# Four feature-major products written token-major, three groups of merged rows turned by VectorE and DRAM, and the last output weights split during the groups before

## The chip, the core and the metric

The kernel runs on one core of one Trainium2 chip. The metric is the device time in microseconds of one execution; lower is better. A time stands for the median of several executions. The profile is of one further execution, whose own time and whose span (first to last instruction of the program) are given with it.

## The reference

One decoder layer over 256 tokens of width 2048, everything in float32:

```python
h = rms_norm(x, norm_w)
proj = h @ w_in                      # 18464 columns
(sb_q, sb_k, sb_v, sb_z, ssd_z, ssd_xbc, ssd_dt, mem_q, mem_z, gate_pre) = split(proj)
o_sb  = stick_breaking_attention(sb_q, sb_k, sb_v) * silu(sb_z)      # 8 heads of 128
x_ssm, b, c = split(silu(causal_conv(ssd_xbc)))
o_ssd = gated_group_rms_norm(ssd_scan(x_ssm, dt, a, b, c) + d * x_ssm, ssd_z)
o_mem = memory_cross_attention(mem_q, rms_norm(mem), w_mem_kv) * silu(mem_z)  # 4 heads of 256
gates = sigmoid(gate_pre + b_gate)
merged = g_sb*(o_sb @ w_branch_sb) + g_ssd*(o_ssd @ w_branch_ssd) + g_mem*(o_mem @ w_branch_mem)
out = rms_norm(x + merged @ w_out, final_norm_w)
```

Nearly all of the work is weight products over 256 tokens: every weight is read from HBM once and used for 256 rows.

## The kernel before

Each product keeps float32 accuracy by splitting both operands into a high and a low part (`split`, lines 140 to 152). ScalarE (ACT) writes the rounded part `wh` from the loaded chunk `raw` (L146), VectorE (DVE) subtracts and writes the rest, `wl` (L150), and TensorE (PE) adds up three products, high by high, high by low and low by high. A chunk of weights is 128 x 1024 numbers, 512 KB, loaded on SyncE's queue (SP) into one of 4 `raw` buffers; `wh` and `wl` have 3 buffers each.

There are two forms of product.

- `gemm` is token-major. The activations are the stationary operand (128 tokens), 512 columns of the weight stream. A chunk is 2 contraction steps of 128 by 512 columns, and PE does 12 matmuls of 512 on it (L266, L267, L268). The result has tokens on partitions.
- `gemm_cols` is feature-major. 128 columns of the weight are stationary and the tokens stream. A chunk is 4 contraction steps by 256 columns. For each step PE does two matmuls of 512 (L229: the high weight by both parts of the activation, side by side) and two of 256 (L233: the low weight). The result has features on partitions, in two halves that `fold` adds up (L246 on ACT, L247 on DVE).

The attention products, the convolution and the scan need features on partitions. For the gates z of each branch the kernel uses `gemm` and turns the result (`to_turned`): DVE transposes 32 x 32 blocks out of PSUM, ACT's queue writes them to a scratch in DRAM and reads them back in four transfers that put the blocks in place. The merged rows, which the output product needs as its stationary operand, are turned by PE (`merged_cols`, L872), eight transposes for each group of 512 columns, into a PSUM bank, from which they are split.

The order of every engine's work is the order in which the program is written (`manual_schedule`). After each chunk's matmuls `pump` counts one step, calls what was put off to this step (`defer(fn, chunks)`) and takes one step of one of two lanes, in which the small work of the attention heads and the scan waits. So "3 chunks later" is a place in the program. An engine works through its own list in order, and ACT issues its DMAs from the same list.

The stages by time: memory values; memory keys (`kT`, feature-major); memory queries (`qM`, feature-major); the gates z of memory and stick-breaking (token-major, turned); stick-breaking queries and keys (`qS`, `kS`, feature-major), during which the memory heads run in the lanes; its values; the scan's z (turned); the convolution's input (feature-major, not touched); then three times four groups of a gate product and a branch product, whose results are added into `merged`; at last four groups of the output product. The first three of these are `gemm`. For the fourth, the code loads and splits all weights first and then runs 48 matmuls of 512 for the first 128 tokens and twice 48 of 256 for the others, so that the end of the kernel is short.

Of the kernel before, what the change touches and what calls it, by code (L numbers as in the profile page):

```python
# [10 lines left out]
F32 = mybir.dt.float32  # L11
F32R = mybir.dt.float32r
# [29 lines left out]
def trunk_kernel(  # L42
# [19 lines left out]
    def nm(s):  # L62
        cnt[0] += 1
        return f"{s}_{cnt[0]}"
# [7 lines left out]
    def ta(shape, n):  # L72
        return tmp.tile(shape, F32, tag="ta", name=nm(n), bufs=4)
# [10 lines left out]
    def small2(shape, n):  # L84
        return tmp.tile(shape, F32, tag="cu", name=nm(n), bufs=2)

# [85 lines left out]
    def defer(fn, chunks=LATE):  # L172

        cnt[0] += 1
        heapq.heappush(late, (now[0] + chunks, cnt[0], fn))
# [72 lines left out]

    def gemm(lhs, nk, w, c0, evac):

        acc2 = psA.tile([P, 2, GW], F32, tag="acc", name=nm("acc"), bufs=2)
        acc = [acc2[:, 0], acc2[:, 1]]
        kc = KC
        for k0 in range(0, nk, kc):
            raw = load_chunk(w, c0, GW, k0, kc)
            wh = stage.tile([P, kc, GW], F32R, tag="wh", name=nm("wh"))
            wl = stage.tile([P, kc, GW], F32R, tag="wl", name=nm("wl"))
            split((wh, wl, raw, None))
            for j in range(kc):
                kt = k0 + j  # L260
                lh, ll = lhs.at(kt)
                first, last = kt == 0, kt == nk - 1
                for t in range(2):
                    a = acc[t]
                    tt = slice(t * P, (t + 1) * P)
                    nc.tensor.matmul(a, lh[:, tt], wh[:, j], start=first, stop=False)  # L266
                    nc.tensor.matmul(a, lh[:, tt], wl[:, j], start=False, stop=False)  # L267
                    nc.tensor.matmul(a, ll[:, tt], wh[:, j], start=False, stop=last)  # L268
            pump()
        defer(lambda: evac(acc))  # L270
# [26 lines left out]

    def to_turned(dst, g):

        scratch = dram.tile([2, P, 4, 4, 32], F32, name=nm("turned"))  # L300
        cols = dst[:, 4 * g:4 * g + 4].rearrange("p k t -> p (k t)").rearrange(
            "p (i n) -> p i n", n=P)

        def evac(acc):
            for t in range(2):
                blocks = ta([P, 4, 4, 32], "blocks")
                nc.vector.transpose(blocks.rearrange("p j k c -> p k j c"),
                                    acc[t].rearrange("p (k j c) -> p k j c", k=4, j=4))
                defer(lambda t=t, blocks=blocks: nc.scalar.dma_start(
                    scratch[t].rearrange("p j k c -> p (j k c)"),  # L310
                    blocks.rearrange("p j k c -> p (j k c)")), 1)
            defer(back, 3)

        def back():
            for j in range(4):
                nc.scalar.dma_start(
                    cols[32 * j:32 * j + 32],
                    scratch[:, :, j].rearrange("t (i r) k c -> r (t i) (k c)", r=32))
        return evac

    def turned(a, i, n=1):
# [134 lines left out]
    def wait_x(k0):  # L456

        assert len(x_ready) >= k0 // 2 + 2, (k0, x_ready)

# [9 lines left out]
    kT = Cols(8, "kT")  # L469
    for g in range(4):  # L470
        gemm_cols(memT, NKT, w_mem_kv, 2 * g * P, to_split_cols(kT, 2 * g),
                  acc=None if g else [bank([P, 2, T], "acc") for _ in range(2)])
    finish()
# [83 lines left out]
    zS = slot([P, 8, T], F32, "zS")  # L557
    for g in range(4):
        gemm_cols(hT, NKT, w_in, C_MEMQ + 2 * g * P, to_split_cols(qM, 2 * g),
                  ready=None if g else wait_x)  # L560
    for dst, c0 in ((zM, C_MEMZ), (zS, C_SBZ)):
# [69 lines left out]
    for dst, c0 in ((qS, C_SBQ), (kS, C_SBK)):  # L631
        for g in range(4):
            gemm_cols(hT, NKT, w_in, c0 + 2 * g * P, to_cols(dst, 2 * g))
    for g in range(2):
# [249 lines left out]
    def branch_evac(br, g, sig):  # L884
        cs = slice(g * GW, (g + 1) * GW)
        def evac(acc):
            for t in range(2):
                if br == 0:
                    nc.vector.tensor_tensor(merged[t][:, cs], acc[t], sig[:, t], ALU.mult)
                else:  # L890
                    nc.vector.tensor_tensor(sig[:, t], acc[t], sig[:, t], ALU.mult)  # L891
                    nc.gpsimd.tensor_tensor(merged[t][:, cs], merged[t][:, cs], sig[:, t],  # L892
                                            ALU.add)
            if br == 2:
                for pr in range(2):
                    defer(lambda pr=pr: merged_cols(4 * g + 2 * pr), 1)
# [62 lines left out]
    def out_evac(g):  # L959
# [4 lines left out]
        return evac  # L964

    for g in range(3):
        gemm(mT[0], NKT, w_out, g * GW, out_evac(g))
# [3 lines left out]
    xr = x_chunk(g)  # L971
    his, los = [], []
    for k0 in range(0, NKT, KC):
        if k0 % 4 == 0:
            his.append(slot([P, 4, GW], F32R, "wlh"))
            los.append(slot([P, 4, GW], F32R, "wll"))
        raw = load_chunk(w_out, g * GW, GW, k0, KC)
        split((his[-1][:, k0 % 4:k0 % 4 + KC], los[-1][:, k0 % 4:k0 % 4 + KC], raw, None))
    drain()
    for t in range(2):  # L980
        tt = slice(t * P, (t + 1) * P)
        for cs in (slice(0, GW),) if t == 0 else (slice(0, T), slice(T, GW)):
            acc = psA.tile([P, 2, GW], F32, tag="acc", name=nm("acc"),
                           bufs=2)[:, 0, 0:cs.stop - cs.start]
            for kt in range(NKT):
# [49 lines left out]
```

## Time and profile before

| | |
|---|---|
| median of 3 executions | 1226.38 us (1225.35 to 1226.67) |
| profiled execution, its own time | 1225.48 us |
| its span | 1223.7 us |
| PE busy in the span | 99% |
| DVE, ACT, POOL busy | 64%, 52%, 4% |
| memory keys: first matmul to that of the next stage | 52.52 to 98.12 us |
| memory queries | 98.12 to 147.11 us |
| memory's and stick-breaking's z | 147.11 to 235.10 us |
| stick-breaking queries and keys | 235.10 to 335.28 us |
| output product, three groups | 1126.51 to 1192.68 us |
| last output group | from 1192.68 us |

PE's matmuls overlap in the records: the time that one adds is read from the distance between two starts, not from its own duration. What ACT, DVE and SP wait for costs nothing by itself; it costs when PE then waits.

### The profile page before, as it was taken

The page shows a single profiled execution, that of the slowest core. Times are in us where ns is not written, and L with a number is a line of the kernel's source. Part 1 is how long each engine was busy: PE and PEld are TensorE (multiplying, and loading weights), DVE is VectorE, ACT ScalarE, POOL GpSimd, SP SyncE. Part 2 cuts the span into 40 slices and gives each one's busy share as a digit, 9 for nine tenths or more (in the row PEclk, how much of TensorE's full clock was granted, in tenths as well). Part 3 has the DMA queues.
Part 4 walks back from the last instruction along what each step waited for, and adds up shares of the span by engine and source line. Part 5 has one row for each costly group of instructions (what it writes and reads, how often), then busy time and mean ns, then how long its engine had stood idle before and what let it go on. Part 6 is the DMA issues. An engine that isn't in the chain of part 4 may idle for free.

```text
span 1223.7 us, 16119 instructions
## 1 busy us (share of the span) xinstructions
PE 1213.0 (99%) x6132; PEld 1024.1 (84%) x6132; DVE 781.5 (64%) x990; ACT 640.7 (52%) x859; POOL 50.4 (4%) x50
## 2 busy tenths in 40 slices
PE   9999999999999999999999999999999999999997
PEld 7888888888888888888888888888888888888886
DVE  5686564556654555888887758676677755555554
ACT  6764533364444444545665757475756544444443
POOL 0000000000000000010100000000000010110101
PEclk9999999999999999999999999999999999999999
DMA  9966578875466778655668667576856666567673
GB/s 308 364 201 191 156 233 230 244 204 155 149 179 189 223 217 232 183 176 177 177 184 221 208 198 222 180 232 180 233 182 189 204 194 210 185 196 243 201 245 112
DMA packets 169646, 251.07 MB, mean 205 GB/s; under 512 B 11040, under 2 KB 85984, under 8 KB 169440
## 3 DMA queue, kind: packets, MB, share of 16 engines
q1 hardware_dynamic: 151840, 229.51, 61.7%
q10 hardware_dynamic: 17728, 20.53, 5.6%
q8 instruction: 48, 0.79, 0.3%
q14 instruction: 30, 0.25, 0.1%
HBM read 243.68 MB, written 6.32 MB: 204 GB/s over the span
## 4 chain that ended last, share of the span: by engine, by line
PE 96%; DMA 1%; issue 1%; ACT 1%; DVE 1%; SPq 0%; POOLq 0%; POOL 0%; ACTq 0%
PE acc L266 20%; PE acc L267 19%; PE acc L268 19%; PE acc L229 19%; PE acc L233 10%; PE acc L429 1%; PE acc L430 1%; PE acc L428 1%; PE y L806 1%; DMA raw<-in_w_out_dram 1%; DMA raw<-in_w_mem_kv_dram 1%; DVE wl L150 0%; PE dtp L490 0%; PE mt L872 0%; PE xp L763 0%
## 5 line engine op out<-in xcount | busy, mean ns | idle before, releaser
L150 DVE TENSOR_TENSOR wl<-raw,wh 128x1024 fp32r<-128x1024 f32 (+1 forms) x409 | 502.8, 1232 | 327.1 <-ACT wh L146 325.1
L146 ACT ACTIVATE wh<-raw 128x1024 fp32r<-128x1024 f32 (+1 forms) x409 | 431.4, 1056 | 417.8 <-PE acc L268 277.6
L229 PE MATMUL acc<-hT,wh 128*128 128x512 f32 x896 | 282.5, 397 | 0.1
L266 PE MATMUL acc<-wh,hT 128*128 128x512 f32 x704 | 276.6, 393 | 0.0
L267 PE MATMUL acc<-wl,hT 128*128 128x512 f32 x704 | 274.3, 390 | 0.0
L268 PE MATMUL acc<-wh,hT 128*128 128x512 f32 x704 | 274.3, 390 | 0.0
L233 PEld LDWEIGHTS acc<-hT,wl 128*128 128x128 f32 x896 | 168.2, 188 | 40.7 <-DVE wl L150 1.0
L233 PE MATMUL acc<-hT,wl 128*128 128x256 f32 x896 | 176.2, 278 | 0.5 <-DVE wl L150 0.5
L268 PEld LDWEIGHTS acc<-wh,hT 128*128 128x128 f32 x704 | 132.2, 188 | 27.9
L266 PEld LDWEIGHTS acc<-wh,hT 128*128 128x128 f32 x704 | 132.2, 188 | 27.3 <-ACT sq L146 0.5
L267 PEld LDWEIGHTS acc<-wl,hT 128*128 128x128 f32 x704 | 132.3, 188 | 26.8 <-DVE wl L150 0.6
L229 PEld LDWEIGHTS acc<-hT,wh 128*128 128x128 f32 x896 | 136.6, 189 | 0.5 <-ACT wh L146 0.3
L266 PE MATMUL acc<-wh,oD 128*128 128x512 f32 x128 | 49.8, 389 | 0.0
L267 PE MATMUL acc<-wl,oD 128*128 128x512 f32 x128 | 49.8, 389 | 0.0
L268 PE MATMUL acc<-wh,oD 128*128 128x512 f32 x128 | 49.8, 389 | 0.0
L720 DVE SCALAR_TENSOR_TENSOR cT<-cu,wcols,cT 128x255 f32<-128x255 f32 (+2 forms) x96 | 46.4, 483 | 3.4
L892 POOL TENSOR_TENSOR merged<-merged,sig 128x512 f32<-128x512 f32 x16 | 25.1, 1590 | 521.5 <-DVE sig L891 521.5
L229 PE MATMUL acc<-memT,wh 128*128 128x512 f32 x128 | 40.5, 398 | 0.0
L266 PE MATMUL acc<-wh,mT 128*128 128x512 f32 x96 | 37.4, 390 | 0.0
L268 PE MATMUL acc<-wh,mT 128*128 128x512 f32 x96 | 37.4, 389 | 0.0
L267 PE MATMUL acc<-wl,mT 128*128 128x512 f32 x96 | 37.4, 389 | 0.0
L233 PEld LDWEIGHTS acc<-memT,wl 128*128 128x128 f32 x128 | 24.0, 188 | 5.9 <-DVE wl L150 0.3
(245 smaller groups left out, 1280.3 us busy)
## 6 DMA issues: line engine op xcount, KB each, us to landing
raw<-in_w_in_dram SPq DMA_DIRECT2D x288, 512.0 KB, 4.2
raw<-in_w_branch_ssd_dram SPq DMA_DIRECT2D x32, 512.0 KB, 4.3
raw<-in_w_out_dram SPq DMA_DIRECT2D x32, 512.0 KB, 4.9
raw<-in_w_mem_kv_dram SPq DMA_DIRECT2D x31, 512.0 KB, 6.2
raw<-in_w_branch_mem_dram SPq DMA_DIRECT2D x16, 512.0 KB, 3.8
raw<-in_w_branch_sb_dram SPq DMA_DIRECT2D x16, 512.0 KB, 4.8
dec<-acT SPq DMA_DIRECT2D x24, 256.0 KB, 6.4
turned<-blocks ACTq DMA_DIRECT2D x16, 256.0 KB, 4.4
```

The lines of the kernel that those rows point to most:

```text
L146: nc.scalar.activation(hi, src, AF.Copy, **({} if scale is None else {"scale": scale}))
L150: nc.vector.tensor_tensor(lo, src, h32, ALU.subtract)
L229: nc.tensor.matmul(halves[b], wh[:, kt - k0, b * P:(b + 1) * P], lhs.both(kt), start=first, stop=False, skip_group_check=True)
L233: nc.tensor.matmul(halves[b][:, 1], wl[:, kt - k0, b * P:(b + 1) * P], lhs.at(kt)[0], start=False, stop=last, skip_group_check=True)
L266: nc.tensor.matmul(a, lh[:, tt], wh[:, j], start=first, stop=False)
L267: nc.tensor.matmul(a, lh[:, tt], wl[:, j], start=False, stop=False)
L268: nc.tensor.matmul(a, ll[:, tt], wh[:, j], start=False, stop=last)
L428: nc.tensor.matmul(a, lh[:, tt], wh[:, g], start=first, stop=False)
L429: nc.tensor.matmul(a, lh[:, tt], wl[:, g], start=False, stop=False)
L430: nc.tensor.matmul(a, ll[:, tt], wh[:, g], start=False, stop=last)
L720: nc.vector.scalar_tensor_tensor(a[:, s:T], u[:, 0:T - s], convw[:, 3 - s, i:i + 1], a[:, s:T], ALU.mult, ALU.add)
L892: nc.gpsimd.tensor_tensor(merged[t][:, cs], merged[t][:, cs], sig[:, t], ALU.add)
```

## The change

1. **Memory's and stick-breaking's queries and keys.** The 16 calls of `gemm_cols` (four for each of `kT`, `qM`, `qS`, `kS`) become 8 calls of `gemm`. Their rows are turned by the path of the gates z, now a general `turning`: DVE transposes both token halves into one tile `blocks`, ACT issues one write of 512 KB one chunk later, the four reads back 2 chunks after that into a tile `turned`, and 3 chunks later this is split (`split_turned`: `kT`, `qM`) or copied (`copy_turned`: `qS`, `kS`). The turned z go through the same code, with one write of 512 KB where there were two of 256 KB.
2. **Merged rows.** Groups 0 to 2 go through `split_turned` from SBUF; only group 3 is still turned by PE.
3. **The last output group.** Its eight chunks of weights are loaded into a tile `early`, one every three chunks of the three groups before, and split two chunks after each load is issued. Its second token half adds up in PSUM banks of the other pool.
4. The assertion on the scaled x follows the smaller contraction step; a small tile of the scan has a tag of its own; the program's `dynamic_dma_scratch_size` is 1024.

```diff
-    def gemm(lhs, nk, w, c0, evac):
+    def gemm(lhs, nk, w, c0, evac, ready=None, acc=None):
...
-    def to_turned(dst, g):
-        scratch = dram.tile([2, P, 4, 4, 32], F32, name=nm("turned"))
...
-                defer(lambda t=t, blocks=blocks: nc.scalar.dma_start(
-                    scratch[t].rearrange("p j k c -> p (j k c)"),
-                    blocks.rearrange("p j k c -> p (j k c)")), 1)
-            defer(back, 3)
+    def turning(use=None, dst=None):
+        scratch = dram.tile([2, P, 4, 4, 32], F32, name=nm("scratch"))
+        def evac(rows):
+            blocks = tmp.tile([P, 2, 4, 4, 32], F32, tag="blocks", name=nm("blocks"), bufs=1)
             for t in range(2):
+                nc.vector.transpose(blocks[:, t].rearrange("p j k c -> p k j c"),
+                                    rows[t].rearrange("p (k j c) -> p k j c", k=4, j=4))
+            defer(lambda: away(blocks), 1)
+        def away(blocks):
+            nc.scalar.dma_start(scratch.rearrange("t p j k c -> p t (j k c)"),
+                                blocks.rearrange("p t j k c -> p t (j k c)"))
+            defer(back, 2)
         def back():
+            cols = dst
+            if dst is None:
+                cols = tmp.tile([P, 8, P], F32, tag="turned", name=nm("turned"), bufs=1)
             for j in range(4):
                 nc.scalar.dma_start(
                     cols[32 * j:32 * j + 32],
                     scratch[:, :, j].rearrange("t (i r) k c -> r (t i) (k c)", r=32))
+            if use is not None:
+                defer(lambda: use(cols), 3)
         return evac
...
+    def split_turned(dst, g):
+        def use(cols):
+            for k in (0, 2):
+                split((*[blocked(a) for a in dst.at(4 * g + k, 2)], tiles(cols, k, 2), None))
+        return turning(use)
+    def copy_turned(dst, g):
+        return turning(lambda cols: nc.scalar.activation(
+            blocked(dst[:, 4 * g:4 * g + 4]), tiles(cols, 0, 4), AF.Copy))
...
-    for g in range(4):
-        gemm_cols(memT, NKT, w_mem_kv, 2 * g * P, to_split_cols(kT, 2 * g),
-                  acc=None if g else [bank([P, 2, T], "acc") for _ in range(2)])
+    for g in range(2):
+        gemm(memT, NKT, w_mem_kv, g * GW, split_turned(kT, g),
+             acc=None if g else [bank([P, GW], "acc") for _ in range(2)])
...
-        gemm_cols(hT, NKT, w_in, C_MEMQ + 2 * g * P, to_split_cols(qM, 2 * g),
+        gemm(hT, NKT, w_in, C_MEMQ + g * GW, split_turned(qM, g),
...
-            gemm_cols(hT, NKT, w_in, c0 + 2 * g * P, to_cols(dst, 2 * g))
+            gemm(hT, NKT, w_in, c0 + g * GW, copy_turned(dst, g))
...
-            if br == 2:
+            if br == 2 and g < 3:
+                defer(lambda: split_turned(mT[0], g)([merged[t][:, cs] for t in range(2)]), 1)
+            elif br == 2:
                 for pr in range(2):
                     defer(lambda pr=pr: merged_cols(4 * g + 2 * pr), 1)
...
+    early = [slot([P, 4, GW], F32, "early")]
+    def ahead(k0):
...
+        ks = slice(k0 % 4, k0 % 4 + KC)
+        raw, hi, lo = early[0][:, ks], his[-1][:, ks], los[-1][:, ks]
+        nc.sync.dma_start(raw, w_out[k0 * P:(k0 + KC) * P, 3 * GW:].rearrange(
+            "(k p) n -> p k n", p=P))
+        defer(lambda: split((hi, lo, raw, None)), 2)
+    for k0 in range(0, NKT, KC):
+        defer(lambda k0=k0: ahead(k0), 1 + 3 * k0 // KC)
...
-            acc = psA.tile([P, 2, GW], F32, tag="acc", name=nm("acc"),
-                           bufs=2)[:, 0, 0:cs.stop - cs.start]
+            if t == 0:
+                acc = psA.tile([P, 2, GW], F32, tag="acc", name=nm("acc"), bufs=2)[:, 0]
+            else:
+                acc = bank([P, T], "acc")
```

How PE's list changes, at the first contraction step of the memory keys, all 512 columns. Before (`acc_523` and `acc_524` are the two column blocks of 128, and a group covers 256 columns; one row of the memory values stands ahead):

```order
L430 MATMUL acc_145<-wh_497,memT_125 128x512
L229 MATMUL acc_523<-memT_122,wh_527 128x512
L229 MATMUL acc_524<-memT_122,wh_527 128x512
L233 MATMUL acc_523<-memT_122,wl_528 128x256
L233 MATMUL acc_524<-memT_122,wl_528 128x256
```

Now (`acc_524` and `acc_525` are the two halves of the tokens, and a group covers 512 columns):

```order
L457 MATMUL acc_145<-wh_497,memT_125 128x512
L269 MATMUL acc_524<-wh_528,memT_122 128x512
L270 MATMUL acc_524<-wl_529,memT_122 128x512
L271 MATMUL acc_524<-wh_528,memT_122 128x512
L269 MATMUL acc_525<-wh_528,memT_122 128x512
L270 MATMUL acc_525<-wl_529,memT_122 128x512
L271 MATMUL acc_525<-wh_528,memT_122 128x512
```

So two matmuls of 512 and two of 256 for 256 columns have become six of 512 for 512 columns, and the low weight is used second, no longer third.

ACT's list in the stick-breaking keys, around the second pair of memory heads. Before (`kS` rows are the folds out of PSUM, `mpr` the heads' exponentials, `mph` a head's split out of PSUM):

```order
L146 ACTIVATE wh_2840<-raw_2838 128x1024
L146 ACTIVATE wh_2864<-raw_2862 128x1024
L246 ACTIVATE kS_2053<-acc_2714 128x512
L587 ACTIVATE mpr_2835,sums_2890<-mpr_2835,nmx_2888 128x256 x2
L146 ACTIVATE wh_2899<-raw_2897 128x1024
L587 ACTIVATE mpr_2860,sums_2923<-mpr_2860,nmx_2921 128x256 x2
L146 ACTIVATE wh_2932<-raw_2930 128x1024
L146 ACTIVATE wh_2960<-raw_2958 128x1024
```

Now (`scratch` rows write the blocks away, `turned` rows read them back):

```order
L313 DMA scratch_2286<-blocks_2575 128x2x512
L146 ACTIVATE wh_2614<-raw_2612 128x1024
L146 ACTIVATE wh_2634<-raw_2632 128x1024
L322 DMA turned_2650<-scratch_2286 32x8x128 x4
L614 ACTIVATE mpr_2610,sums_2659<-mpr_2610,nmx_2657 128x256 x2
L146 ACTIVATE wh_2668<-raw_2666 128x1024
L614 ACTIVATE mpr_2630,sums_2688<-mpr_2630,nmx_2686 128x256 x2
L146 ACTIVATE wh_2697<-raw_2695 128x1024
L146 ACTIVATE wh_2721<-raw_2719 128x1024
L345 ACTIVATE kS_1929<-turned_2650 128x1024
```

The fold ahead of the exponentials has gone; in its place stand the four reads back, and the copy of 1024 comes two chunks after the exponentials.

ACT's list in the first output group, now (`wlh` rows are the last group's weights, from `early`; before, all eight `wlh` stood behind the three groups):

```order
L146 ACTIVATE wh_9222<-raw_9220 128x1024
L146 ACTIVATE wlh_9199<-early_9177 128x1024
L146 ACTIVATE wh_9246<-raw_9244 128x1024
L146 ACTIVATE wh_9275<-raw_9273 128x1024
L146 ACTIVATE wh_9293<-raw_9291 128x1024
L146 ACTIVATE wlh_9199<-early_9177 128x1024
L146 ACTIVATE mT_8083<-mt_9263 128x2x256
L146 ACTIVATE mT_8083<-mt_9268 128x2x256
L146 ACTIVATE wh_9317<-raw_9315 128x1024
```

One more split of a chunk stands behind every third chunk, the second of them right ahead of the split of the fourth group's merged columns.

More of the change, by code (lines that the diff above doesn't have):

```diff
@@ L84, in small2 @@
     def small2(shape, n):
-        return tmp.tile(shape, F32, tag="cu", name=nm(n), bufs=2)
+        return tmp.tile(shape, F32, tag="cbs", name=nm(n), bufs=2)
     def bank(shape, n="bank"):
@@ L247, in fold @@
             nc.vector.tensor_tensor(dst, acc[:, :, 0], dst, ALU.add)
-    def gemm(lhs, nk, w, c0, evac):
-        acc2 = psA.tile([P, 2, GW], F32, tag="acc", name=nm("acc"), bufs=2)
-        acc = [acc2[:, 0], acc2[:, 1]]
+    def gemm(lhs, nk, w, c0, evac, ready=None, acc=None):
+        if acc is None:
+            acc2 = psA.tile([P, 2, GW], F32, tag="acc", name=nm("acc"), bufs=2)
+            acc = [acc2[:, 0], acc2[:, 1]]
         kc = KC
         for k0 in range(0, nk, kc):
+            if ready is not None:
+                ready(k0)
             raw = load_chunk(w, c0, GW, k0, kc)
@@ L318, in back, with quarter, tiles, to_turned @@
                     scratch[:, :, j].rearrange("t (i r) k c -> r (t i) (k c)", r=32))
-        return evac
+            if use is not None:
+                defer(lambda: use(cols), 3)
+        return evac
+    def quarter(a):
+        return a.rearrange("p k t -> p (k t)").rearrange("p (i n) -> p i n", n=P)
+    def tiles(cols, k, n):
+        return cols.rearrange("p i (k c) -> p k i c", c=32)[:, k:k + n]
+    def to_turned(dst, g):
+        return turning(dst=quarter(dst[:, 4 * g:4 * g + 4]))
+    def split_turned(dst, g):
[6 more added lines that the diff above has]
+            blocked(dst[:, 4 * g:4 * g + 4]), tiles(cols, 0, 4), AF.Copy))
     def turned(a, i, n=1):
@@ L456, in wait_x @@
     def wait_x(k0):
-        assert len(x_ready) >= k0 // 2 + 2, (k0, x_ready)
+        assert len(x_ready) >= k0 // 2 + 1, (k0, x_ready)
     head = tb([P, NKT + T], "head")
@@ L557, in trunk_kernel @@
     zS = slot([P, 8, T], F32, "zS")
-    for g in range(4):
-        gemm_cols(hT, NKT, w_in, C_MEMQ + 2 * g * P, to_split_cols(qM, 2 * g),
-                  ready=None if g else wait_x)
+    for g in range(2):
+        gemm(hT, NKT, w_in, C_MEMQ + g * GW, split_turned(qM, g),
+             ready=None if g else wait_x)
     for dst, c0 in ((zM, C_MEMZ), (zS, C_SBZ)):
@@ L631, in trunk_kernel @@
     for dst, c0 in ((qS, C_SBQ), (kS, C_SBK)):
-        for g in range(4):
-            gemm_cols(hT, NKT, w_in, c0 + 2 * g * P, to_cols(dst, 2 * g))
+        for g in range(2):
+            gemm(hT, NKT, w_in, c0 + g * GW, copy_turned(dst, g))
     for g in range(2):
@@ L964, in out_evac @@
         return evac
+    his, los = [], []
+    early = [slot([P, 4, GW], F32, "early")]
+    def ahead(k0):
+        if k0 % 4 == 0:
+            his.append(slot([P, 4, GW], F32R, "wlh"))
+            los.append(slot([P, 4, GW], F32R, "wll"))
+        ks = slice(k0 % 4, k0 % 4 + KC)
[5 more added lines that the diff above has]
+        defer(lambda k0=k0: ahead(k0), 1 + 3 * k0 // KC)
     for g in range(3):
@@ L971, in trunk_kernel @@
     xr = x_chunk(g)
[L972 to L978, printed above, removed]
     drain()
@@ L1022 @@
     from concourse.bass_utils import run_bass_kernel_spmd as _run
-    nc = _bacc.Bacc("TRN2", target_bir_lowering=False, num_devices=1)
+    nc = _bacc.Bacc("TRN2", target_bir_lowering=False, num_devices=1,
+                     dynamic_dma_scratch_size=1024)
     arrays, args = {}, []
```

6 lines of the change are left out of this document (removed).

## The prediction

> **What bounds the kernel now.** I read the page first, then what PE waits for, then PE's rows stage by stage.
>
> ```profile
> span 1223.7 us, 16119 instructions
> PE 1213.0 (99%) x6132; PEld 1024.1 (84%) x6132; DVE 781.5 (64%) x990; ACT 640.7 (52%) x859; POOL 50.4 (4%) x50
> PE 96%; DMA 1%; issue 1%; ACT 1%; DVE 1%; SPq 0%; POOLq 0%; POOL 0%; ACTq 0%
> PE warm L110 <- POOL ones L99: 1.1, 1, 1.1
> PE acc L233 <- DVE wl L150: 0.5, 1, 0.5
> PE acc L428 <- ACT memT L146: 0.5, 1, 0.5
> PE acc L429 <- DVE wl L150: 0.3, 1, 0.3
> ```
>
> PE is the bound from start to end: the chain of work that ended last is 96% PE, and its recorded waits add up to 2.4 us. So a change counts by what it takes off PE's own list, plus any wait that it makes or removes. Everything else is cover.
>
> **Term A: the form of the product.** What a matmul costs in a stream is the distance between starts. These rows are the first and last of two undisturbed stretches, feature-major and token-major.
>
> ```profile
> 500.22 0.63 PE L229 MATMUL acc<-hT,wh 128*128 128x512 f32 x2
> 507.19 0.62 PE L229 MATMUL acc<-hT,wh 128*128 128x512 f32 x2
> 199.74 0.39 PE L266 MATMUL acc<-wh,hT 128*128 128x512 f32 x1
> 213.34 0.39 PE L266 MATMUL acc<-wh,hT 128*128 128x512 f32 x1
> 500.22:507.19 6.97, 6.97 (x43) 1.00 0.50 152
> 199.74:213.34 13.60, 13.60 (x62) 1.00 0.93 263
> ```
>
> From 500.22 to 507.19 there are ten steps of two matmuls of 512 and two of 256: 0.697 us for one contraction step of 256 columns. From 199.74 to 213.34 there are 60 matmuls of 512: 0.2267 us each, and three of them do the same step: 0.680. Both stream 1536 rows, so what differs is a small cost for each matmul (four instead of three). The change converts 4 products of 4 groups of 16 steps, 256 steps: 256 x 0.017 = **4.35 us** less. The clock reads 1.00 in both stretches.
>
> The Trainium skill (TensorE: Matmul & The Clock Gate, "Back-to-back issue gap") gives 518 cycles for 512 rows and 262 for 256 at 2.4 GHz, about 216 and 109 ns; by it a step would be an estimated 0.650 against 0.648 us and term A would be 0.5 us. The rows here, 0.697 and 0.680, disagree with it, and they are what I use; the case is a rival below.
>
> **Term B: the transposes.** Three pieces of the last branch stage, 96 matmuls of 512 each, the third with eight transposes in it:
>
> ```profile
> 949.74:971.50 21.76, 21.76 (x97) 18.02 (x96) 16.86 (x21) 11.69 (x16) 2.72 (x2) 1.00 0.63 206
> 993.26:1015.92 22.66, 22.66 (x105) 18.85 (x104) 12.72 (x12) 9.46 (x10) 3.53 (x2) 1.00 0.60 190
> L307 DVE STREAM_TRANSPOSE blocks<-acc 128x512 f32<-128x512 f32 x16 | 10.4, 690 | 0.0
> ```
>
> A group of transposes costs PE 22.66 - 21.76 = 0.90 us; three groups go: **2.70 us**. In their place DVE gets two transposes of 0.69 for each group. They wait for POOL's addition into `merged`, and the next weight split stands behind them on DVE; DVE was busy 12.72 of 22.66 us there, so some 9.9 us cover 1.4 us and that wait.
>
> **Term C: the stall in the stick-breaking keys.**
>
> ```profile
> 318.39 1.06 ACT L146 ACTIVATE wh<-raw 128x1024 fp32r<-128x1024 f32 x1 [3.17 <-PE acc L229]
> 322.85 0.60 ACT L246 ACTIVATE kS<-acc 128x512 f32<-128x512 f32 x1 [3.40 <-PE acc L233]
> 325.00 0.51 ACT L587 ACTIVATE mpr<-mpr,nmx 128x256 f32<-128x256 f32 x1 [1.55 <-DVE nmx L584]
> 329.14 0.51 ACT L587 ACTIVATE mpr<-mpr,nmx 128x256 f32<-128x256 f32 x1 [2.09 <-DVE nmx L584]
> 330.14 2.94 ACT L146 ACTIVATE wh<-raw 128x1024 fp32r<-128x1024 f32 x3
> 330.78 0.40 PE L233 MATMUL acc<-hT,wl 128*128 128x256 f32 x2
> 331.23 0.73 PE L229 MATMUL acc<-hT,wh 128*128 128x512 f32 x2
> 332.49 0.50 PE L233 MATMUL acc<-hT,wl 128*128 128x256 f32 x2 [0.53 <-DVE wl L150]
> ```
>
> ACT ran ahead, met the fold of `kS`, and stood 3.40 us for PE to finish the group. Then came two waits for the memory heads' exponentials, DVE behind them, and `wh` at 330.14 was late: PE's step from 331.23 takes 1.26 to 332.49 where two matmuls of 512 take 0.47, so 0.8 us at this spot, and the step ahead of it (330.78 to 331.23, two matmuls of 256) is 0.2 too long as well: 1.0 and a little more. The change removes the fold: the rows are evacuated by DVE, a chunk later than before, and ACT meets the four reads back instead. They cost ACT issue time (1.89 us, below) while DVE prepares the same exponentials. Bounds: a gain of 1.1 when the 3.40 us of lead comes back, and a loss of about the same when the reads wait for the write. I take a gain of **0.9**, nearer the first, because the wait that goes is longer than what comes.
>
> **Term D: the tail.**
>
> ```profile
> 1203.06 0.68 DVE L919 TENSOR_TENSOR yo<-acc,xr 128x512 f32<-128x512 f32 x1
> 1203.34 0.39 PE L990 MATMUL acc<-wlh,mT 128*128 128x512 f32 x1
> 1203.80 0.39 PE L988 MATMUL acc<-wlh,mT 128*128 128x256 f32 x1
> ...
> 1215.29 0.28 PE L990 MATMUL acc<-wlh,mT 128*128 128x256 f32 x1
> ```
>
> The last group's second half needs the PSUM buffer of the third group, whose evacuation stands on DVE behind the eight late splits and ends at 1203.74. PE starts 0.46 after the last start instead of 0.23: **0.23 us**. With the banks of the other pool, and the splits done earlier, it goes. The work behind the last matmul is untouched: PE starts its last matmul at 1215.29, and the span ends 8.4 us later. No load of the eight was on PE's path, so splitting them early gains nothing else.
>
> **What is added, and its cover.** The turn is already in the kernel, eight times. One of them, and the landings:
>
> ```profile
> 169.08 1.06 ACT L146 ACTIVATE wh<-raw 128x1024 fp32r<-128x1024 f32 x1 [1.66 <-PE acc L268]
> 172.05 0.93 ACTq L309 DMA_DIRECT2D turned<-blocks  x2
> 178.50 1.89 ACTq L316 DMA_DIRECT2D zM<-turned  x4
> turned<-blocks ACTq DMA_DIRECT2D x16, 256.0 KB, 4.4
> zT<-turned ACTq DMA_DIRECT2D x16, 128.0 KB, 6.3
> 147.11:235.10 87.99, 87.99 (x395) 72.87 (x393) 49.57 (x67) 34.96 (x34) 0.46 (x1) 1.00 0.80 233
> ```
>
> On ACT's list behind the write stand two chunks (2.72 us each) and then the reads; the write lands in 4.4 us of 6.45, and the reads (6.3) have three chunks, 8.2 us, before their use. ACT idles 1.66 us in each chunk for a free `wh` buffer, so the 1.89 us of issuing uses up one such gap. In this stage of 87.99 us, in which the turns of z begin, PE was busy throughout, and 384 matmuls of 0.2267 alone take 87.04. I cost eight more product turns and three merged ones at 0; uncovered they would cost ACT's issuing, 11 x 1.89 = 21 us. One write of 512 KB replaces two in flight together, so its landing lies between 4.4 and twice that. At 8.8 us ACT would stand about 2.4 us, and it is two chunks ahead, 5.4 us less the 1.06 of its own split: still covered.
>
> The early splits add 1.06 us on ACT and 1.23 on DVE to every third chunk:
>
> ```profile
> 1176.39 3.24 DVE L150 TENSOR_TENSOR wl<-raw,wh 128x1024 fp32r<-128x1024 f32 x2 [1.75 <-ACT wh L146]
> 1174.88 2.54 POOL L922 TENSOR_TENSOR yo<-yo,fw 128x512 f32<-128x512 f32 x2 [19.20 <-ACT junk L921]
> 1126.51:1192.68 66.17, 66.17 (x297) 54.88 (x296) 37.36 (x33) 29.77 (x36) 8.63 (x6) 1.00 0.70 228
> ```
>
> DVE is busy 37.36 of 66.17 us there and gets 8 x 1.23 more, 47 of 66. The tight place is behind an evacuation, where two splits took 3.24 instead of 2.46 with POOL at work. SP's queue carries eight more loads between the weights' own: 15.1 MB become at most 19.3 in 65 us, which scales the DMA share from 0.70 to at most 0.91. Zero, with a loss of up to 1 us.
>
> One place loses: at the start of the memory keys.
>
> ```profile
> 54.54 1.21 DVE L150 TENSOR_TENSOR wl<-raw,wh 128x1024 fp32r<-128x1024 f32 x1
> 55.80 0.50 PE L233 MATMUL acc<-memT,wl 128*128 128x256 f32 x2
> ```
>
> The low part ends at 55.75 and is used at 55.80. It stood third on PE's list and now stands second, 0.23 us earlier: a loss of **0.2** (0 to 0.5).
>
> **Sum.** 4.35 + 2.70 + 0.9 + 0.23 - 0.2 = 8.0 us. The profiled execution took 1225.48 (span 1223.7): 1217.5, span 1215.7. The median of the executions shown is 0.9 above the profiled one, which would give 1218.4; I put 1218.0.
>
> **Rivals.**
> - *The attention stage keeps its stall, or gets one.* The reads wait for a slow write just where the memory heads take ACT's lead (2.09 and 1.55 us of waits above). Term C turns to -1.1 and the gain to 6.0: 1220.0. For it: `wl` ends 0.05 us before its use around 331 already.
> - *The output stage becomes tight.* If each of eight early splits makes PE wait 0.5 us, 4 us come back: 1222.0. For it: 3.24 us of DVE beside POOL. Against: it needs it eight times, and only two evacuations fall there.
> - *Term A is not the form's.* If the 0.017 belongs to the stage of the convolution and not to the matmuls, the gain is 3.65: 1222.3. Against: four starts a step instead of three is a property of the list. The Trainium skill's cycle table, cited above, would have this outcome.
> - *The return from DRAM is late, and the kernel slower.* One mechanism: ACT's four reads wait for the write, and the next `wh` stands behind them. PE waits once a write takes over 5.4 + 4.3 = 9.7 us. To eat 8.0 us and 2.5 more over 11 turns, each must cost 0.95, a landing of some 10.7; at 11.6, 11 x 1.9 = 21 us: 1239. Against: 4.4 us measured. The Trainium skill (VectorE: DVE Perf Modes, "The three transpose paths") speaks for this rival: it calls a plain DMA with strides for the transpose 19 times slower than the crossbar's and recommends TensorE for 128 x 128. The landings of 4.4 and 6.3 us show no such slowness for this layout.
>
> **How the numbers follow.** Forecast, 1216.5 to 1219.5: 0.63. Attention stage: 0.18. Output stage: 0.07. Term A absent: 0.03. A gain that nothing shows, by several small waits: 0.05. Slower: 0.04. The range from 1216.0 to 1221.5 holds the forecast and the first rival. A measurement of this kernel tells about 0.2%, 2.45 us, from no change: faster (below 1223.9) 0.91, within 0.06, slower 0.03.
>
> **What would show it.** Stages from first matmul to first matmul: memory keys 45.6 to about 43.7, stick-breaking queries and keys 100.2 to about 98; a gate product with turned rows 21.76 instead of 22.66; no PE wait near 331; the step into 256-column matmuls 0.23. Wrong: `acc` matmuls that wait for DVE `wl` or ACT `wh` behind `turned` rows, writes landing over 9 us, or 0.697 us a step where `gemm` now stands.

## The result, and the profile after

The changed kernel takes 1217.66 us (median of 6 executions, 1217.49 to 1219.59), the kernel before, run beside it, 1225.68 (6 executions, 1225.35 to 1226.67): a ratio of 0.9937, 95% interval 0.9924 to 0.995. The forecast was 1218.0 (1216.0 to 1221.5). The profiled execution took 1217.57 us.

The page of the changed kernel, its first lines and the chain by engine, and what PE waited for:

```profile
span 1215.8 us, 15596 instructions
PE 1204.7 (99%) x5852; PEld 1008.3 (83%) x5852; DVE 784.7 (65%) x995; ACT 636.1 (52%) x846; POOL 49.6 (4%) x50
PE 93%; DMA 3%; ACT 1%; issue 1%; DVE 1%; ACTq 0%; SPq 0%; POOLq 0%; POOL 0%; DVEq 0%
PE acc L455 <- ACT memT L146: 1.3, 2, 1.0
PE warm L110 <- POOL ones L99: 1.1, 1, 1.1
PE acc L456 <- DVE wl L150: 0.4, 1, 0.4
PE acc L270 <- DVE wl L150: 0.3, 2, 0.2
```

PE is still the bound. The wait for the low part in `gemm_cols` (line 233), which stood in the attention stage, is gone; new in the list is a wait for the low part in `gemm` (line 270), 0.3 us. (The attention stage is that of the stick-breaking queries and keys.)

Stage by stage, first matmul to first matmul, in the two profiled executions:

| stage | before, us | after, us | difference |
|---|---|---|---|
| up to the memory keys (same code) | 52.52 | 51.89 | -0.63 |
| memory keys | 45.60 | 44.89 | -0.71 |
| memory queries | 48.98 | 48.59 | -0.40 |
| gates z of memory and stick-breaking | 87.99 | 87.98 | -0.01 |
| stick-breaking queries and keys | 100.18 | 97.15 | -3.03 |
| values, scan's z, convolution | 327.95 | 327.91 | -0.04 |
| branch stages | 463.28 | 460.59 | -2.69 |
| output product to PE's last matmul | 89.06 | 88.73 | -0.33 |

Stretches of the changed kernel (time, PE, PEld, DVE, ACT and POOL busy, clock, DMA share, GB/s): memory keys, stick-breaking queries and keys, a gate product of the last branch, the three output groups:

```profile
51.89:96.78 44.89, 44.71 (x197) 36.72 (x196) 33.40 (x46) 24.08 (x34) 0.89 (x2) 1.00 0.84 241
233.35:330.50 97.15, 97.15 (x469) 81.78 (x468) 56.55 (x70) 48.88 (x61) 0.00 (x0) 1.00 0.77 216
988.44:1010.20 21.76, 21.76 (x97) 18.02 (x96) 12.84 (x13) 9.54 (x10) 3.53 (x2) 1.00 0.83 241
1119.00:1185.18 66.18, 66.18 (x297) 54.90 (x296) 44.10 (x38) 34.27 (x40) 8.64 (x6) 1.00 0.72 244
```

The gate product beside the merged rows is 21.76 us, like one without transposes. The three output groups take 66.18, as before, with DVE at 44.10 instead of 37.36. The attention stage has no idle PE in it.

ACT's list at the place of the old stall, and PE's step into the last 48 matmuls:

```profile
315.35 1.82 ACTq L322 DMA_DIRECT2D turned<-scratch  x4
319.37 0.51 ACT L614 ACTIVATE mpr<-mpr,nmx 128x256 f32<-128x256 f32 x1 [2.99 <-DVE nmx L611]
323.50 0.51 ACT L614 ACTIVATE mpr<-mpr,nmx 128x256 f32<-128x256 f32 x1 [2.09 <-DVE nmx L611]
1195.84 0.39 PE L1030 MATMUL acc<-wlh,mT 128*128 128x512 f32 x1
1196.06 0.28 PE L1028 MATMUL acc<-wlh,mT 128*128 128x256 f32 x1
```

The reads are issued while ACT would in any case wait for the exponentials (2.99 us), so their 1.82 us cost nothing. PE steps into the 256-column matmuls after 0.22 us.

One new wait was not in the sum. ACT, DVE and PE at the start of the memory queries, and the DMA issues of the turns (count, KB each, median us to landing):

```profile
95.83 1.15 ACT L146 ACTIVATE kT<-turned 128x512 fp32r<-128x512 f32 x2 [2.19 <-DMA turned<-scratch]
98.76 1.23 DVE L150 TENSOR_TENSOR wl<-raw,wh 128x1024 fp32r<-128x1024 f32 x1 [0.18 <-ACT wh L146]
99.50 0.39 PE L269 MATMUL acc<-wh,hT 128*128 128x512 f32 x1
100.04 0.50 PE L270 MATMUL acc<-wl,hT 128*128 128x512 f32 x1 [0.15 <-DVE wl L150]
scratch<-blocks ACTq DMA_DIRECT2D x19, 512.0 KB, 4.8
turned<-scratch ACTq DMA_DIRECT2D x44, 128.0 KB, 6.8
DMA to landing us min/median/max: 4.6/6.8/11.8
```

The write of 512 KB lands in 4.8 us where 256 KB took 4.4, as assumed. But a read can take 11.8 us, more than the 8.2 of its three chunks. Then ACT stands at the *use* of the rows, the low part of the next weights ends at 99.99, and PE's second matmul starts 0.54 us after the first instead of 0.23.

### The profile page after: what moved, and what is told of

Read it like the earlier page. It is cut to its first block, busy times and chain, and to the rows that moved or that the text cites. A ratio compares the mean times of both kernels' runs of the same rounds, so it can differ in the third digit from the quotient of the medians.

```text
span 1215.8 us, 15596 instructions
## 1 busy us (share of the span) xinstructions
PE 1204.7 (99%) x5852; PEld 1008.3 (83%) x5852; DVE 784.7 (65%) x995; ACT 636.1 (52%) x846; POOL 49.6 (4%) x50
## 4 chain that ended last, share of the span: by engine, by line
PE 93%; DMA 3%; ACT 1%; issue 1%; DVE 1%; ACTq 0%; SPq 0%; POOLq 0%; POOL 0%; DVEq 0%
PE acc L269 24%; PE acc L270 24%; PE acc L271 24%; PE acc L229 10%; PE acc L233 5%; DMA raw<-in_w_mem_kv_dram 1%; PE y L833 1%; DMA turned<-scratch 1%; DMA rows<-in_mem_dram 1%; DVE wl L150 1%; ACT wh L146 1%; PE acc L456 0%; PE acc L457 0%; PE dtp L517 0%; PE acc L1030 0%
## 5 line engine op out<-in xcount | busy, mean ns | idle before, releaser
L269 PE MATMUL acc<-wh,hT 128*128 128x512 f32 x896 | 351.5, 392 | 0.0
L270 PE MATMUL acc<-wl,hT 128*128 128x512 f32 x896 | 349.2, 390 | 0.2 <-DVE wl L150 0.2
L271 PE MATMUL acc<-wh,hT 128*128 128x512 f32 x896 | 349.0, 390 | 0.0
L271 PEld LDWEIGHTS acc<-wh,hT 128*128 128x128 f32 x896 | 168.2, 188 | 35.4
L270 PEld LDWEIGHTS acc<-wl,hT 128*128 128x128 f32 x896 | 168.3, 188 | 34.8 <-DVE wl L150 1.1
L269 PEld LDWEIGHTS acc<-wh,hT 128*128 128x128 f32 x896 | 168.3, 188 | 34.6 <-issue 0.5
L229 PE MATMUL acc<-hT,wh 128*128 128x512 f32 x512 | 161.5, 397 | 0.0
L233 PEld LDWEIGHTS acc<-hT,wl 128*128 128x128 f32 x512 | 96.2, 188 | 22.7
L233 PE MATMUL acc<-hT,wl 128*128 128x256 f32 x512 | 100.7, 278 | 0.0
L229 PEld LDWEIGHTS acc<-hT,wh 128*128 128x128 f32 x512 | 78.0, 189 | 0.1
L270 PEld LDWEIGHTS acc<-wl,oD 128*128 128x128 f32 x128 | 24.0, 188 | 5.0
L271 PEld LDWEIGHTS acc<-wh,oD 128*128 128x128 f32 x128 | 24.0, 188 | 5.0
```

What stands on the lines that cost most here:

```text
L229: nc.tensor.matmul(halves[b], wh[:, kt - k0, b * P:(b + 1) * P], lhs.both(kt), start=first, stop=False, skip_group_check=True)
L233: nc.tensor.matmul(halves[b][:, 1], wl[:, kt - k0, b * P:(b + 1) * P], lhs.at(kt)[0], start=False, stop=last, skip_group_check=True)
```

## The experiments

All times beside runs of the kernel before on the same chip.

**The two halves of the change.** The product form alone (merged rows turned by PE, late splits, old bank), and everything but the form (the sixteen `gemm_cols` back).

```diff
 # product form alone
-            if br == 2 and g < 3:
-                defer(lambda: split_turned(mT[0], g)([merged[t][:, cs] for t in range(2)]), 1)
-            elif br == 2:
+            if br == 2:
... (and the last output group as in the kernel before)
 # all but the form, the same for qM, qS, kS
-    for g in range(2):
-        gemm(memT, NKT, w_mem_kv, g * GW, split_turned(kT, g),
+    for g in range(4):
+        gemm_cols(memT, NKT, w_mem_kv, 2 * g * P, to_split_cols(kT, 2 * g),
```

> Only the queries and keys are written token-major and turned; merged rows and the last output group are as before. If the forecast's terms are right in size, 4.35 (form) + 0.9 (stall in the stick-breaking keys) - 0.2 (start of the memory keys) = 5.05 us less than the kernel before. If the stages of the changed kernel's trace are the better account (memory keys -0.7, memory queries -0.4, stick-breaking queries and keys -3.0), 4.1 us less, and the wait near 99 us at the start of the memory queries is there again. If the form is worth nothing (rival), about 0.9 less. In all cases the three gate products with transposes still take 22.66 us.

> The changed kernel with the queries and keys feature-major again: only the merged rows and the last output group are changed. Theory: 2.70 + 0.23 = 2.9 us less than the kernel before, with the stages up to the convolution as before (memory keys 45.6, memory queries 49.0, stick-breaking queries and keys 100.2) and the stall near 331 us back. Rival: the early splits make PE wait in the output stage, and the gain is under 2 us.

The form alone: 1221.14 us against 1225.79, ratio 0.9958 (0.9941 to 0.9975). All but the form: 1222.16, ratio 0.9971 (0.996 to 0.9982). The gains, 4.65 and 3.63 us, add up to 8.3, the change's 8.0 within their spread, so nothing shows that the parts touch each other. The form's own terms (4.35 + 0.9 - 0.2) made 5.05, the others (2.70 + 0.23) 2.93. The 4.65 lies between these 5.05 and the 4.1 of the stages and can't tell them apart. The wait near 99 us, expected again in the form alone, did not come: its memory queries took 48.15 us.

The form alone, its attention stage and its step into the last matmuls:

```profile
233.60:330.75 97.15, 97.15 (x470) 81.81 (x468) 56.56 (x70) 48.94 (x61) 0.00 (x0) 1.00 0.76 214
1198.78 0.39 PE L1017 MATMUL acc<-wlh,mT 128*128 128x512 f32 x1
1199.67 0.38 PE L1015 MATMUL acc<-wlh,mT 128*128 128x256 f32 x1 [0.50 <-DVE yo L946]
```

All but the form, a gate product beside merged rows and the place of the old stall:

```profile
992.93:1014.69 21.76, 21.76 (x98) 18.02 (x97) 12.85 (x13) 9.54 (x10) 3.54 (x2) 1.00 0.85 242
330.89 0.73 PE L229 MATMUL acc<-hT,wh 128*128 128x512 f32 x2
332.15 0.50 PE L233 MATMUL acc<-hT,wl 128*128 128x256 f32 x2 [0.53 <-DVE wl L150]
```

Each effect goes with its part: 97.15 with the form; 21.76 and no transposes with the turned merged rows; the stall near 331 (1.26 us from start to start) stays with the old form. The old tail costs 0.89 - 0.23 = 0.66 us in the first of these executions, more than the 0.23 that the one trace of before showed.

**Was it the fold?** The kernel before, with the folds of `qS` and `kS` one chunk later, nothing else.

```diff
-            gemm_cols(hT, NKT, w_in, c0 + 2 * g * P, to_cols(dst, 2 * g))
+            gemm_cols(hT, NKT, w_in, c0 + 2 * g * P, to_cols(dst, 2 * g), late=3)
... (and the new argument in gemm_cols)
```

> The kernel before, with the folds of the stick-breaking queries and keys three chunks behind their group and no longer two; nothing else. Theory (the fold took ACT's lead): ACT no longer stands 3.4 us for PE ahead of the memory heads' exponentials, the 1.26 us step near 331 us goes back to 0.47, and the stage of 100.18 us takes 99.1 to 99.4. Rival (the memory heads' own waits make the stall): the stage stays at 100.2.

It took 1223.61 us once. Its attention stage and ACT's list there:

```profile
234.00:333.06 99.06, 99.06 (x597) 87.68 (x596) 57.28 (x71) 49.39 (x65) 0.00 (x0) 1.00 0.64 178
321.63 0.51 ACT L587 ACTIVATE mpr<-mpr,nmx 128x256 f32<-128x256 f32 x1 [3.27 <-DVE nmx L584]
323.58 0.57 ACT L246 ACTIVATE kS<-acc 128x512 f32<-128x512 f32 x1
326.36 0.51 ACT L587 ACTIVATE mpr<-mpr,nmx 128x256 f32<-128x256 f32 x1 [2.21 <-DVE nmx L584]
```

Behind the first pair of exponentials the fold no longer waits for PE, its 3.40 us are gone, and PE's idle time with them: 100.18 becomes 99.06. So the stall was the fold's place in ACT's list, and it was worth 1.1 us, the upper end of the prediction's bounds. The form then accounts for 99.06 - 97.15 = 1.91 us of this stage.

**The tail: bank or early splits?** One kernel with the old PSUM pool and early splits, one with the new bank and late splits.

```diff
 # old bank, early splits (the other edit, not shown, splits the last group behind the three others again)
-            if t == 0:
-                acc = psA.tile([P, 2, GW], F32, tag="acc", name=nm("acc"), bufs=2)[:, 0]
-            else:
-                acc = bank([P, T], "acc")
+            acc = psA.tile([P, 2, GW], F32, tag="acc", name=nm("acc"),
+                           bufs=2)[:, 0, 0:cs.stop - cs.start]
```

> The changed kernel with the last group's second half back in the PSUM pool of the first, the early splits kept. Theory 1 (what made PE wait at the step into the 256-column matmuls was the third group's evacuation standing on DVE behind the eight late splits; with the splits early it is done in time, and the other bank is not needed): the step from the last 512-column matmul to the first of 256 is 0.23 us and the time that of the changed kernel, 1217.7 us. Rival (only the other bank removes the wait): the step is 0.46 us, as in the kernel before, or up to 0.92, as with the product form alone, and the time 0.2 to 0.7 us more, which only the step itself can show.

> The changed kernel with the last group's weights split late, behind the three groups, as in the kernel before; its second half keeps the bank of the other pool. Theory 1 (the bank alone is enough, and splitting early gains nothing else): the step into the 256-column matmuls is 0.23 us, PE has no wait at the start of the last group, and the time is 1217.7 us. Rival A (the early splits are what helps): the step is 0.46 to 0.92 us. Rival B (the late loads do cost PE something at the start of the last group, and the early ones removed it): a wait ahead of the last group's first matmuls. In the output stage the lead of the low parts behind an evacuation, 0.31 us in the changed kernel, goes back to 0.8 us.

1217.59 and 1217.93 us, once each; spans 1215.6 and 1215.5. PE's step with the old bank, then with the late splits:

```profile
1195.67 0.39 PE L1028 MATMUL acc<-wlh,mT 128*128 128x512 f32 x1
1195.89 0.28 PE L1026 MATMUL acc<-wlh,mT 128*128 128x256 f32 x1
```

```profile
1195.47 0.39 PE L1021 MATMUL acc<-wlh,mT 128*128 128x512 f32 x1
1195.69 0.28 PE L1019 MATMUL acc<-wlh,mT 128*128 128x256 f32 x1
```

0.22 us in both, in one execution each: either edit removes the wait, and the second one then buys nothing. The early splits were not needed, and they seem to have a price: the three output groups took 66.17 or 66.18 us in all four executions with late splits, and 66.18 to 66.81 in the nine with early ones.

**Use of the rows 5 chunks after the reads, not 3.**

```diff
-                defer(lambda: use(cols), 3)
+                defer(lambda: use(cols), 5)
```

> The changed kernel with the split or copy of turned rows five chunks behind the reads, no longer three. Theory (the reads land later than the 8.2 us allowed, and ACT stands for them at 95.8, 121.2 and 143.0 us): those waits of 2.2, 3.5 and 2.0 us go, the 0.4 us that PE loses near 99.5 us goes, and the memory queries take 48.1 to 48.2 us and no longer 48.59. Rival (the split of x and of the memory keys is simply much work for ACT and DVE there): the stage stays at 48.6.

1218.29 us once, not better. At the memory keys' rows ACT now stands no more, and the memory queries take 48.07 us. But with 3 chunks they took 48.07 to 48.21 in the other executions too, and 48.59 in that one: a late read reaches PE only now and then. Meanwhile this execution lost more elsewhere, at the start of the memory keys, where nothing was changed. ACT, DVE and PE there, and ACT's first use of the keys' rows:

```profile
51.49 0.63 ACT L381 ACTIVATE rows<-rows 128x512 f32<-128x512 f32 x1 [0.48 <-DMA rows<-in_x_dram]
54.72 1.22 DVE L150 TENSOR_TENSOR wl<-raw,wh 128x1024 fp32r<-128x1024 f32 x1
54.42 0.44 PE L269 MATMUL acc<-wh,memT 128*128 128x512 f32 x1
55.99 0.50 PE L270 MATMUL acc<-wl,memT 128*128 128x512 f32 x1 [1.13 <-DVE wl L150]
98.83 1.13 ACT L146 ACTIVATE kT<-turned 128x512 fp32r<-128x512 f32 x2
```

PE's second matmul comes 1.57 us after the first. The low part stands on DVE behind the splitting of the values, and ACT's part of that stands behind the statistics of x, whose rows were still landing at 51.49.

**No chunk between the write and the reads.**

```diff
-            defer(back, 2)
+            defer(back, 0)
```

> The changed kernel with the four reads back issued right behind the write, with no chunk between them, so that they wait for the landing of the write on ACT's list. Theory (the return from DRAM is hidden only by its place in the list): ACT stands for the 4.8 us of the write's landing and 1.9 us of issuing, 6.7 us, against 1.7 us of its own idle time in each chunk and some 3.2 us that the low parts are ahead; so PE waits about 1.8 us at most of the 19 turns, 15 to 35 us in all: 1233 to 1253 us, with PE waiting for DVE wl or ACT wh behind the reads. Rival 1 (ACT is two chunks ahead and makes it up): a PE wait of under 0.5 us each, 1217 to 1227 us. Rival 2 (the reads do not hold the list, they wait on their queue): no wait of PE, 1217.7 us.

1257.95 us: 40.4 us more than the change, 2.1 us for each of the 19 turns, above the theory's 15 to 35. One of them, in the memory queries, from the chain of waits (start, us, what), then PE's list, then one stretch (time, PE, PEld, DVE, ACT and POOL busy, clock, DMA share, GB/s):

```profile
157.27 5.39 DMA scratch<-blocks
162.69 0.32 ACTq L322
164.61 1.06 ACT wh L146
165.70 1.24 DVE wl L150
163.53 0.39 PE L271 MATMUL acc<-wh,hT 128*128 128x512 f32 x1
165.72 0.50 PE L269 MATMUL acc<-wh,hT 128*128 128x512 f32 x1 [1.79 <-ACT wh L146]
166.98 0.80 PE L270 MATMUL acc<-wl,hT 128*128 128x512 f32 x1 [0.76 <-DVE wl L150]
167.60:169.60 2.00, 2.00 (x6) 1.61 (x5) 1.90 (x6) 1.00 (x2) 0.00 (x0) 0.50 0.75 183
```

The chain is the one that the prediction's slower rival named: landing 5.39, four reads to issue, high part, low part, and PE late by 1.96 and 1.03 us. Then comes something that no theory had: matmuls of 512 start 0.43 us apart, not 0.23, and the granted clock reads 0.50. In this execution 25 matmuls behind four turns ran so, 5 us in all. Without them the loss is 35 us, the theory's upper end. So the turn is free only by its place in the program; its cover, two chunks, is worth 40 us.

**The convolution as rows too**: all eight groups; six of eight (the edit shown); four of eight.

```diff
-        for j in range(2):
-            gemm_cols(hT, NKT, w_in, C_XBC + g * GW + 2 * j * P, conv_evac(4 * g + 2 * j))
+        if i < 6:
+            gemm(hT, NKT, w_in, C_XBC + g * GW, conv_evac(4 * g, True))
+        else:
+            for j in range(2):
+                gemm_cols(hT, NKT, w_in, C_XBC + g * GW + 2 * j * P, conv_evac(4 * g + 2 * j))
```

> The changed kernel with the convolution's input converted too: its sixteen products of 256 columns become eight of 512, turned by the same path and copied out; the taps read the copy. Theory 1 (the four matmuls a step cost 0.017 us more than three, wherever they stand): another 256 steps x 0.017 = 4.35 us less, the convolution's stage 188.5 to 184.2 us, the time 1213.3 us, a ratio of about 0.990 to the kernel before. Rival 1 (DVE, busy over 80% there with the taps, becomes late with the low parts): PE waits for DVE wl, and some or all of the gain is lost: 1214 to 1222 us. Rival 2 (the 0.017 us belongs to the stage and not to the form): the stage stays at 188.5, 1217.7 us.

1224.29 us, ratio 0.9985 (0.9975 to 0.9994): most of the change's gain lost, and more than the rival of a late DVE allowed (1214 to 1222). The profiled execution, 1226.07 us, was the slowest of the ten. The first six groups of the changed kernel, then of this one:

```profile
469.90:613.75 143.85, 143.85 (x833) 126.24 (x832) 117.47 (x181) 76.53 (x94) 7.38 (x4) 1.00 0.63 184
```

```profile
469.24:610.21 140.97, 140.97 (x641) 117.57 (x640) 105.45 (x156) 75.48 (x88) 5.73 (x4) 1.00 0.78 224
656.07 1.06 ACT L743 ACTIVATE cu<-turned 128x1024 f32<-128x1024 f32 x1 [3.64 <-DMA turned<-scratch]
```

2.88 us less over 192 steps, 0.0150 a step: the cost of the fourth matmul belongs to the form and not to the stage. But the last two groups lose 1.3 us and the branch stages 10.0. The rows come back some chunks later than a fold out of PSUM (a whole group must end, then the write, two chunks, the reads, three more), so the taps of the last groups fall into the scan, where ACT stands 3.64 us for them. How much of the 10.0 us is due to that is not shown: this version also has one buffer for the copies, where the next two have four, and puts off the last `silu` longer, and 3.41 us of this execution ran at half the clock (last section).

> The changed kernel with the first six of the convolution's eight groups as rows, turned by the same path, and the last two groups feature-major as before; the copies for the taps have four buffers of 256 columns instead of two. Theory (the gain of the form is there in each converted group, 0.45 to 0.5 us measured in each of the first six when all eight were converted; the waits at the end of that kernel came from the last two groups, whose rows come back from DRAM, and whose taps run, just when the scan needs them): the six groups keep 24.25, 23.2, 23.0, 24.4, 21.9 and 24.25 us, the last two 22.37 and 22.29, the branch stages their 460.6 us: 2.9 us less than the changed kernel, 1214.8 us, about 0.991 of the kernel before. Rival (the waits do not belong to the last groups: wherever the form is token-major beside the taps, DVE or ACT get late by the end of the stage): PE waits for DVE wl in the seventh group or in the scan's first stage, and the time is 1217 us or more.

1218.4 us, ratio 0.9936 (0.9924 to 0.9949), against 1218.08 for the unaltered change on the same chip: no difference. The six groups kept their 2.9 us, but the eighth took 25.54 instead of 22.29, and the branch stages 461.33 instead of 460.59. The time is the rival's (1217 or more), and so is the cause, low parts that come late from DVE; but the wait stood mainly in the eighth group, where the rival had not put it.

> As the version with six converted groups of the convolution, but only the first four; the last four groups stay feature-major. Theory (with six, the rows of the sixth group came back late in the stage, so that its four taps and those of the seventh group fell into the same eight chunks: DVE then has 1.22 us of splitting and 1.93 of taps in every chunk, 3.15 where PE needs 2.79, and was late for eight chunks on end; with four, the same overlap falls into the fifth group, and PE waits again there by about the same, 8 x 0.36 = 2.9 us less the 3.2 us that the low parts are ahead, so 0 to 2 us, but three groups remain in which DVE gets its lead back): the first four groups 0.45 to 0.5 us shorter, 1.9 us together, a wait of 0 to 2 us in the fifth, none in the seventh, eighth or in the scan: 1215.8 to 1217.8 us. Rival (the wait of the version with six came from the scan's start, not from the overlap): no wait in the fifth group and again 2 to 4 us lost at the end of the stage, 1218 us or more.

1221.6 us, ratio 0.9963 (0.9951 to 0.9974). The sixth group of this kernel, then of the changed one:

```profile
586.41:613.45 27.04, 25.83 (x147) 21.46 (x145) 26.15 (x47) 14.62 (x16) 0.00 (x0) 1.00 0.55 156
```

```profile
589.02:613.75 24.73, 24.73 (x146) 21.76 (x145) 20.05 (x31) 16.48 (x19) 0.00 (x0) 1.00 0.64 188
```

The four converted groups gain 1.9 us, and the wait moves with the change of form: the fifth group has none, the sixth and seventh (24.66 for 22.37) lose 2.3 each, the eighth and the scan nothing. So it is not the scan's start: DVE, with the taps of two groups in its list at once, is busy for 26.15 of 27.04 us, where it had 20.05 of 24.73. Its size, put at 0 to 2 us in the fifth group, was wrong: 4.6, and later. No version here beats the change.

**The change once more**, beside the version with six groups.

> The changed kernel itself, unaltered, once more, beside the version with six converted groups and on the same chip. Expected: 1217.7 us, a ratio of 0.9937; the waits at the start of the memory keys and of the memory queries come again in other sizes (0 to 1.5 us), since they hang on when the rows of x and the turned rows land.

1218.08 us (1217.22 to 1218.24), ratio 0.9931 (0.9917 to 0.9944). Memory keys 45.57, memory queries 48.16, the attention stage again 97.15, the branch stages 460.60. The gates z took 88.15 here, where every other execution of this form but the one with the reads at once has 87.98. Most of what differs between the executions lies in the first 146 us.

## Why the prediction was right

- **The bound.** A change counted by what it took off PE's list; the stage differences sum to 7.84 us, and the span fell by 7.9. The forecast sum was 8.0. By stages its terms made 0.89 us for the memory keys, 1.09 for the memory queries, 3.08 for the stick-breaking queries and keys, 2.70 for the branches and 0.23 for the end; the traced execution gave 0.71, 0.40, 3.03, 2.69 and 0.33, and 0.63 ahead of them all.
- **Term A**, the form: sign and cause right, size too large. It was put at 0.017 us a step, from two undisturbed stretches. Whole stages show 0.0150: 2.88 us over 192 steps of the convolution, 1.91 over the attention stage's 128. For 256 steps that makes an estimated 3.8, not 4.35. In the attention stage the `gemm` matmuls are 0.2278 us apart on average, where the undisturbed stretch has 0.2267: 0.4 us over 384 of them. Why they are was not followed up.
- **Term B**, the transposes: 463.28 to 460.59, 2.69 against 2.70.
- **Term C**, the stall: put at 0.9, it measured 100.18 - 99.06 = 1.1. The mechanism, the fold in ACT's list, is shown by moving the fold alone. The rival of an attention stage that keeps its stall did not come: the reads went into ACT's wait for the exponentials.
- **Term D**, the tail: 0.23 in the traced execution. Two others with late splits and the old bank had 0.66 (the form alone) and 0.69 (folds later), so the term was read from one favourable execution.
- **Added turns and early splits at 0.** Right for the turns after the first 150 us: the gates z kept 87.98, and the last branch lost nothing. The output stage kept 66.18 in the traced execution, but others with early splits lost up to 0.6 us in it. With the old bank one low part came 0.35 us late there (start to start, two steps). So that rival's place is real, and its size at most a sixth of the 4 us given.
- **The loss at the start of the memory keys**, 0.2 (0 to 0.5): the mechanism was right, its bounds were not. The second matmul came late by 0.34 us in the changed kernel's profile and by 0 to 1.35 in its variants, since the low part waits for work behind DMA landings and not for PE. There "PE is the bound from start to end" failed: what PE saves ahead of this place is lost at it. In the nine executions with converted memory products and reads in their place, the gates z begin at 144.66 to 145.68 us, mean 145.1; in the three without, at 146.01 to 147.11, mean 146.6: 1.5 us gained of 2.18 - 0.2. Of these 1.5, 0.3 lie ahead of the memory keys, in code that is the same, so the two products themselves gave 1.2.
- **Late return from DRAM** was put at the reads, waiting for a slow write. The write was as assumed; the reads were late, up to 11.8 us, at the use of the rows. It cost 0.4 us in one execution.
- **Three slips**: the text expected the memory keys to go to about 43.7. Its own terms give 45.6 - 1.09 + 0.2 = 44.7; measured were 44.89, and 44.6 to 45.9 in the variants with the reads in their place. It expected about 98 for the stick-breaking queries and keys, where its terms give 100.18 - 2.18 - 0.9 = 97.1; measured were 97.15. And its estimate of 0.5 us for term A, by the cycles that it cites, is 0.6 when nothing is rounded on the way.

So the total was right partly by luck: term A was 0.5 too large and the starts of two stages lost more than put, while terms C and D gave more and the start of the program, which is the same code, was 0.6 faster in the traced execution.

## What to carry to other kernels

Where PE is the bound, count starts on its list: four matmuls where three do the same work cost 0.015 us a step here, and a transpose taken off PE gave back its whole time. The round trip through DRAM was free here because ACT, which issues it, had waits to spend, for a free buffer or for DVE, and only by its place: two chunks less cost 40 us, and the delay of the round trip pushed the taps of a convolution into work that had no room. Where an engine that works in order waits for something late, look at whether moving that one instruction does the same as a rewrite: one chunk for a fold gained 1.1 us.

## What the runs showed of the hardware

PE's clock fell after some of its waits. With the reads at once, behind 1.96 and 1.03 us of waits from 163.5 us on, matmuls of 512 started 0.427 us apart instead of 0.227, from 167.57 to 169.70, at a granted clock of 0.50. With all of the convolution as rows, behind 2.20 and 1.03 us, the same for 3.3 us from 679.5.

The length of the waits alone does not decide it. With the reads at once PE waited 1.52 and 1.03 us near 88 us, and the clock stayed; it waited about as long near 114, and the clock fell. The difference is when they came. The four stretches at half the clock in this execution are each 3.41 us long and start at 115.34, 166.54, 217.74 and 316.72 us, so they lie 15, 15 and 29 times 3.413 us apart, on one fixed beat. On this beat the waits near 88 us fall into two windows, those near 114 into one (time, PE, PEld, DVE, ACT and POOL busy, clock, DMA share, GB/s):

```profile
84.62:88.03 3.41, 2.48 (x11) 1.70 (x10) 0.00 (x0) 0.68 (x1) 0.00 (x0) 1.00 1.08 212
88.03:91.44 3.41, 2.21 (x8) 1.61 (x9) 3.00 (x4) 2.47 (x5) 0.00 (x0) 1.00 0.79 126
91.44:94.85 3.41, 3.41 (x17) 2.82 (x16) 3.41 (x6) 3.41 (x6) 0.00 (x0) 1.00 0.86 273
111.93:115.34 3.41, 1.23 (x7) 0.67 (x6) 1.48 (x2) 2.56 (x3) 0.00 (x0) 1.00 0.51 99
115.34:118.75 3.41, 3.41 (x9) 2.64 (x9) 3.22 (x4) 1.43 (x3) 0.00 (x0) 0.50 0.72 207
```

Between 10 and 1220 us of this execution, PE was busy for 0.66 to 1.30 us in the four windows ahead of half the clock, and for 1.97 us or more in every other one. With all of the convolution as rows it was 0.92 us ahead of the one fall and 2.25 or more in every other window. Where between 1.30 and 1.97 us the border lies, no run shows.

The Trainium skill (TensorE: Matmul & The Clock Gate, "What's actually happening") says that the array runs at half or full rate by how busy it was in a free-running window of about 3.4 us. The trace agrees on the half rate, the length of 3.41 us and the fixed beat. So a wait of PE can have a second price, about 0.2 us for each matmul that follows in that time: here up to 1.6 us on top of 3.
